# Expert and mixer weights as tiles with 16 KB per partition row, and the pools that hold them

## The chip, the core and the metric

The kernel runs on one core of one Trainium2 chip. The metric is the device time of one execution in microseconds (us); three executions before the change are shown. Times inside the kernel come from one profiled execution.

## What is computed

256 tokens of width 1024 pass through two blocks. The first block is a mixer (half a Hyena convolution, half a differential attention), and then a mixture of experts in which each of 16 experts picks its 32 tokens. Cut to what matters here, the reference's expert part is:

```
cap = EC_CAPACITY_FACTOR * L // N_EXPERTS      # 32
aff = jax.nn.softmax(logits, axis=-1)
g, idx = lax.top_k(aff.transpose(2, 0, 1), cap)
xin = h[bi, idx]
a = jnp.einsum('bcd,df->bcf', xe, wg)          # d 1024, f 2816, for each expert
u = jnp.einsum('bcd,df->bcf', xe, wu)
y = jnp.einsum('bcf,fd->bcd', jax.nn.silu(a) * u, wd)
```

The experts' weights are 16 x 3 x 1024 x 2816 values of float32, 554 MB, each used once. The second block (two layers: gated feed-forward, a mixer, a second feed-forward, a gated embedding) has some 180 MB of weights for all 256 tokens.

## The kernel before, in words

**Weight tiles.** All large weights come as tiles of 128 partitions x 2048 float32, 8 KB per partition and 1 MB per load, packed on the host so that a tile is contiguous in HBM. `load_w` (L125) takes a slot from the list `K.raws` (L119, the one taken longest ago) and issues one load on SP's queue (L131). A slot is free again when its last reader is done. For the mixers and the second block, `split_w` (L150) parts a tile into float32r high and low parts: ScalarE copies (L162), VectorE or GpSimd subtracts (L165), in two pieces of 1024 columns that go to slots of the pools `hl`, `hlf` and others; each product is then three matmuls (`mm3`, L182 to L184). The experts' weights are multiplied as they are, in float32.

**First mixers** (`pre` L800, `mixers` L844). The projection `w_in` is 6 blocks of 512 columns, two tiles each (half of the 1024 rows per tile); `weights(n)` (L922) fetches both. The first five tiles are fetched ahead (L866, L874), in between small tables. `w_out` is four tiles (L822). SBUF is two stacks, left and right. On the left lie `raw` (3 slots) and `rawx` (2 slots), then the pools of the mixers; when these are done, the right stack gets `rx` and `rawy` (NY = 12 slots, L813), and the first 12 expert tiles are fetched into it (L814); 4 more follow when `rawz1` (2 slots, L1109) opens.

**Experts** (`moe` L1103). Four quartets q of experts, and in each 11 chunks c of 256 features: 44 chunks. The 32 tokens of each of the four experts stand on 32 of 128 PSUM partitions, so that the four experts' matmuls (stationary 128 x 32, moving 128 x 512) stand side by side. A chunk loads 8 gate and up tiles (expert e, half h of the rows) and 4 down tiles (expert e), 12 MB. The order on TensorE is

```
for h in range(2):
    w = [K.load_w(("moe_gu", 4 * q + e, c, h)) for e in range(4)]
    for k in range(4):
        for e in range(4):
            ...
```

so the first product of a half needs the tiles of all four experts, and the four slots come free together (L1122 to L1128). Each `nc.tensor.matmul` of float32 is two instructions in the profile. Then ScalarE takes the SiLU (L1139), VectorE multiplies (L1140), TensorE transposes (L1144), and the down products follow (L1146 to L1151), again with the expert innermost. The router (L971) finds the tokens before; the pairs of k of the gathered tokens `xinT` (L1035) come one after another, and the first products are woven in between.

**Slots.** In quartets 0 to 2 the list holds 3 + 2 + 12 + 2, and from the first chunk on one more (`rawz`, L1135): 20 slots of 8 KB. At the start of quartet 3 (L1157) the right stack's pools close, `rawz` is closed and opened anew with one slot, and 8 slots stay; the room goes to tables of the second block's S5 layer, which are worked out in six parts behind the first six chunks (L1170 to L1175; VectorE L331 and others, TensorE L466 and L497, small transfers L473 from GpSimd's queue). Behind chunk 5 the tables' scratch closes and `rawz2` gives 4 more (L1178). At the end of a quartet the outputs are put back to their tokens (L1182 to L1190).

**Second block** (`second` L1654). It uses the 3 slots of `raw`, which have been there from the beginning. Its first step splits a feed-forward tile (L1659), its second is `final_norm` (L1200, ScalarE's square on L1209).

**Who orders what.** The order on each engine and in each queue follows the order of the program, except that the language's scheduler moves instructions and loads that are ready earlier ahead of others: the first expert tiles, for instance, go to free slots of `rawx` and `raw` before those of `rawy`. `issue_after` (L148, L1174) holds an instruction behind another.

## Time and profile before

| | us |
|---|---|
| three executions | 2633.45, 2632.69, 2639.59 |
| median | 2633.45 |
| profiled execution: span from first to last instruction | 2637.2 |
| profiled execution: what lies around the span | not listed |
| to the first expert products | about 228 |
| experts | 228 to 1536 |
| second block | 1536 to the end |
| TensorE busy (matmul) | 2168.1, 82% of the span |
| VectorE, ScalarE, GpSimd busy | 922.9, 627.2, 112.2 |

The span is read in stages, since a mean over stages with different limits says little: where the sixteen DMA engines are busy all the time, bytes count, and where TensorE is, instructions count. The groups of rows below are from the page of this execution and from queries of its trace. [...] SPq is SyncE's load queue.

### The profile page before, as it was taken

What the parts mean: (1) busy time and instruction counts of PE and PEld (TensorE: products, weight loads), DVE (VectorE), ACT (ScalarE), POOL (GpSimd) and SP (SyncE); (2) the same over time, 40 slices, a digit from 0 to 9 for tenths busy, and PEclk for the clock granted to TensorE, in tenths of its full rate; (3) what the DMA queues carried; (4) which work ended last, traced back from release to release, by engine and by line L of the source; (5) the groups of instructions that cost most, each with busy time, mean ns of one, the idle gap of its engine ahead of it and who ended that gap; (6) DMA issues with size and microseconds to landing.
All of it is one profiled execution on the core that took longest, in us unless ns stands there. A gap on an engine that the chain in (4) does not pass through costs nothing.

```text
span 2637.2 us, 26475 instructions
## 1 busy us (share of the span) xinstructions
PE 2168.1 (82%) x10570; PEld 1199.1 (45%) x10570; DVE 922.9 (35%) x1745; ACT 627.2 (24%) x966; POOL 112.2 (4%) x85
## 2 busy tenths in 40 slices
PE   7997767666767767676677689999999999899998
PEld 5763111111111111111122157778777777777776
DVE  6653000000000000002412055565754755686545
ACT  4421000000000000000000044443543544465443
POOL 1110000000000000000000010001000200100001
PEclk9998898999899898988888889999999999899999
DMA  5248999999999999999998975533654554344541
GB/s 204 98 170 346 421 420 420 421 421 420 421 420 420 420 421 420 420 394 421 421 361 357 422 292 189 185 119 121 250 190 146 192 192 180 128 160 150 189 164 44
DMA packets 108002, 761.68 MB, mean 289 GB/s; under 512 B 12343, under 2 KB 12648, under 8 KB 17240
## 3 DMA queue, kind: packets, MB, share of 16 engines
q1 hardware_dynamic: 107000, 757.60, 72.1%
q0 software_dynamic: 880, 2.40, 0.5%
q8 instruction: 83, 1.36, 0.2%
q14 instruction: 39, 0.32, 0.0%
HBM read 757.72 MB, written 1.05 MB: 288 GB/s over the span
## 4 chain that ended last, share of the span: by engine, by line
DMA 45%; PE 45%; DVE 7%; ACT 1%; issue 1%; SPq 0%; POOL 0%; DVEq 0%; ACTq 0%; POOLq 0%
DMA w<-in_moe_gu 29%; DMA w<-in_moe_d 16%; PE b_w L184 8%; PE b_w L182 8%; PE b_w L183 8%; PE b_y L182 3%; PE b_y L184 3%; PE b_y L183 3%; PE b_au L1127 2%; DVE wlo L165 1%; PE b_y L1149 1%; PE b_pj L183 1%; PE b_pj L184 1%; PE b_pj L182 1%; PE b_tr L1300 1%
## 5 line engine op out<-in xcount | busy, mean ns | idle before, releaser
L1127 PE MATMUL b_au<-w,xinT 128*32 128x512 f32 x2816 | 611.5, 729 | 282.6 <-DMA w<-in_moe_gu 282.4
L165 DVE TENSOR_TENSOR wlo<-w,whi 128x1024 fp32r<-128x1024 f32 (+2 forms) x354 | 427.0, 1213 | 239.9 <-ACT whi L162 233.2
L1127 PEld LDWEIGHTS b_au<-w,xinT 128*32 128x32 f32 x2816 | 123.2, 128 | 734.9 <-DMA w<-in_moe_gu 497.3
L162 ACT ACTIVATE whi<-w 128x1024 fp32r<-128x1024 f32 (+2 forms) x374 | 385.4, 1040 | 248.0 <-PE b_w L184 131.7
L1140 DVE SCALAR_TENSOR_TENSOR m_g<-b_au,rsg,m_g 128x256 f32<-128x256 f32 x44 | 21.3, 483 | 1101.2 <-ACT m_g L1139 1101.2
L182 PE MATMUL b_w<-whi,hT 128*128 128x512 f32 (+2 forms) x864 | 347.1, 402 | 1.4 <-ACT hT L254 0.8
L184 PE MATMUL b_w<-whi,hT 128*128 128x512 f32 (+2 forms) x864 | 341.1, 395 | 2.7 <-DVE hT L255 2.7
L183 PE MATMUL b_w<-wlo,hT 128*128 128x512 f32 (+2 forms) x864 | 340.1, 394 | 0.9 <-DVE wlo L165 0.9
L1149 PE MATMUL b_y<-w,m_gT 128*32 128x512 f32 x1408 | 294.2, 602 | 53.4 <-DMA w<-in_moe_d 32.6
L1139 ACT ACTIVATE m_g<-b_au,rsg 128x256 f32<-128x256 f32 x44 | 20.8, 473 | 1215.6 <-PE b_au L1127 1215.6
L184 PEld LDWEIGHTS b_w<-whi,hT 128*128 128x128 f32 x864 | 164.5, 190 | 40.0 <-DVE hT L255 5.3
L182 PEld LDWEIGHTS b_w<-whi,hT 128*128 128x128 f32 x864 | 165.3, 191 | 34.9 <-ACT hT L254 2.9
L183 PEld LDWEIGHTS b_w<-wlo,hT 128*128 128x128 f32 x864 | 164.9, 191 | 33.6 <-DVE wlo L165 1.9
L1149 PEld LDWEIGHTS b_y<-w,m_gT 128*32 128x32 f32 x1408 | 69.9, 109 | 237.9 <-issue 124.2
L184 PE MATMUL b_y<-whi,f_gT 128*128 128x512 f32 x352 | 139.6, 401 | 7.9 <-DVE f_gT L255 7.9
L182 PE MATMUL b_y<-whi,f_gT 128*128 128x512 f32 x352 | 145.9, 414 | 0.0
L183 PE MATMUL b_y<-wlo,f_gT 128*128 128x512 f32 x352 | 140.7, 400 | 0.0
L165 POOL TENSOR_TENSOR wlo<-w,whi 128x1024 fp32r<-128x1024 f32 (+1 forms) x20 | 48.1, 2415 | 1004.4 <-ACT whi L162 819.6
L184 PEld LDWEIGHTS b_y<-whi,f_gT 128*128 128x128 f32 x352 | 66.9, 192 | 32.6 <-DVE f_gT L255 17.9
L182 PEld LDWEIGHTS b_y<-whi,f_gT 128*128 128x128 f32 x352 | 67.0, 190 | 29.8 <-ACT f_gT L254 19.3
L183 PEld LDWEIGHTS b_y<-wlo,f_gT 128*128 128x128 f32 x352 | 67.2, 191 | 10.3
L255 DVE TENSOR_TENSOR f_gT<-b_tr,f_gT 128x256 fp32r<-128x256 f32 x88 | 37.0, 421 | 64.0 <-ACT f_gT L254 64.0
(535 smaller groups left out, 1917.4 us busy)
## 6 DMA issues: line engine op xcount, KB each, us to landing
w<-in_moe_gu SPq DMA_DIRECT2D x352, 1024.0 KB, 19.8
w<-in_moe_d SPq DMA_DIRECT2D x176, 1024.0 KB, 19.8
w<-in_ffn_gu SPq DMA_DIRECT2D x88, 1024.0 KB, 4.8
w<-in_ffn_d SPq DMA_DIRECT2D x44, 1024.0 KB, 4.8
w<-in_w_in SPq DMA_DIRECT2D x12, 1024.0 KB, 8.3
w<-in_ab_in SPq DMA_DIRECT2D x8, 1024.0 KB, 4.8
w<-in_ple_g SPq DMA_DIRECT2D x8, 1024.0 KB, 4.8
w<-in_w_out SPq DMA_DIRECT2D x4, 1024.0 KB, 5.0
```

The source lines that it names most:

```text
L162: nc.scalar.activation(hi, s, AF.Copy)
L165: (e or nc.vector).tensor_sub(lo, s, hi.bitcast(F32))
L182: mm(out, lh, rh, start=start, stop=False)
L183: mm(out, lh, rl, start=False, stop=False)
L184: mm(out, ll, rh, start=False, stop=stop)
L255: return self.nc.vector.tensor_sub(lo, src, hi.bitcast(F32)), i
L1127: nc.tensor.matmul(au[e * 32:(e + 1) * 32], xinT[:, h * 4 + k, s:s + 32], w[e][:, k * 512:(k + 1) * 512], start=h + k == 0, stop=h == 1 an ...
L1139: nc.scalar.activation(g, au[:, :256], AF.Silu, scale=r)
L1140: v.scalar_tensor_tensor(g, au[:, 256:], r, g, op0=ALU.mult, op1=ALU.mult)
L1149: mm = nc.tensor.matmul(y[n][e * 32:(e + 1) * 32], gT[:, f, e * 32:(e + 1) * 32], w[e][:, f * 1024 + n * 512:f * 1024 + (n + 1) * 512], st ...
L1300: nc.tensor.transpose(b[:, f * 128:(f + 1) * 128], g[:, f * 128:(f + 1) * 128], K.ident)
```

## The change

It makes the experts' and the first mixers' tiles twice as wide, 16 KB per partition and 2 MB per load. An expert tile now holds the same rows for all four experts of a quartet: a gate and up tile two values of k (256 of the 1024 rows), a down tile one of the two groups of 128 features. Every tile can so be multiplied as soon as it is there. A chunk has 4 + 2 loads in place of 8 + 4. `w_in` has one tile per block of columns, of which the first is loaded in two parts; `w_out` has two tiles. The pools change with it: `rawx` has 3 slots of 16 KB and lives until the experts are done, `rawy` 6, `rawz1` 1, `rawz` 1 from quartet 3 on, `rawz2` 2; `raw`, with 3 slots of 8 KB, opens only for the second block, under the pool `post`. GpSimd's scratch for its own DMA descriptors is cut to 4096 bytes per partition; nothing is named before, and the default is 16384. Lines that only change comments are left out.

```diff
-NY = 12
+NY = 6
...
-        self.add_raw(ctx.enter_context(self.pool("raw", raw_bufs)), raw_bufs)
+        self.cols = 2048
...
+    @contextmanager
+    def width(self, cols):
+        old, self.cols = self.cols, cols
+        yield
+        self.cols = old
...
-        return p.tile([128, 2048], F32, name="w")
+        return p.tile([128, self.cols], F32, name="w")
...
-    def load_w(self, key, cols=2048):
+    def load_w(self, key, cols=None, parts=1):
...
-        self.nc.sync.dma_start(t[:, :cols], src[key[1:]] if len(key) > 1 else src)
+        src = src[key[1:]] if len(key) > 1 else src
+        n = (cols or self.cols) // parts
+        for i in range(parts):
+            c = slice(i * n, (i + 1) * n)
+            self.nc.sync.dma_start(t[:, c], src[:, c])
...
-        n = cols // 2
+        cols = cols or self.cols
+        m = max(2, cols // 1024)
+        n = cols // m
         parts = ([], [])
-        for i in range(2):
+        for i in range(m):
             p = self.hls.pop(0)
...
             for h in (1, 0):
+                w = K.weight(("w_out", h))
                 for n in range(2):
-                    w = K.weight(("w_out", n, h))
...
-    K.prefetch([("w_in", 2, 0), ("w_in", 2, 1)])
+    K.prefetch([("w_in", 2)], parts=2)
...
-    K.prefetch([("w_in", 3, 0), ("w_in", 3, 1), ("w_in", 4, 0)])
+    K.prefetch([("w_in", 3), ("w_in", 4)])
...
     def weights(n):
-        return [K.weight(("w_in", n, h)) for h in range(2)]
+        return K.weight(("w_in", n))
...
-            K.prefetch([("w_out", n, h) for h in (1, 0) for n in range(2)])
+            K.prefetch([("w_out", h) for h in (1, 0)])
...
-        rz1.enter_context(K.more_raw("rawz1", 2))
+        rz1.enter_context(K.more_raw("rawz1", 1))
...
-            for h in range(2):
-                w = [K.load_w(("moe_gu", 4 * q + e, c, h)) for e in range(4)]
-                for k in range(4):
+            for k2 in range(4):
+                w = K.load_w(("moe_gu", q, c, k2))
+                for i in range(2):
+                    k = 2 * k2 + i
                     for e in range(4):
                         s = q * 128 + e * 32
-                        nc.tensor.matmul(au[e * 32:(e + 1) * 32], xinT[:, h * 4 + k, s:s + 32],
-                                         w[e][:, k * 512:(k + 1) * 512], start=h + k == 0, stop=h == 1 and k == 3)
+                        o = (2 * e + i) * 512
+                        nc.tensor.matmul(au[e * 32:(e + 1) * 32], xinT[:, k, s:s + 32], w[:, o:o + 512],
+                                         start=k == 0, stop=k == KT - 1)
...
-                rz.enter_context(K.more_raw("rawz", 13 - NY, last=True))
-            w = [K.load_w(("moe_d", 4 * q + e, c)) for e in range(4)]
+            w = [K.load_w(("moe_d", q, c, f)) for f in range(2)]
...
                     for e in range(4):
+                        o = e * 1024 + n * 512
                         mm = nc.tensor.matmul(y[n][e * 32:(e + 1) * 32], gT[:, f, e * 32:(e + 1) * 32],
-                                              w[e][:, f * 1024 + n * 512:f * 1024 + (n + 1) * 512],
-                                              start=c + f == 0, stop=c == NCH - 1 and f == 1)
+                                              w[f][:, o:o + 512], start=c + f == 0, stop=c == NCH - 1 and f == 1)
...
                     right.close()
-                    rz.close()
                     rz.enter_context(K.more_raw("rawz", 1))
...
-                    rz.enter_context(K.more_raw("rawz2", 4, last=True))
+                    rz.enter_context(K.more_raw("rawz2", 2, last=True))
...
-    K = Core(ctx, tc, raw_bufs=3)
+    K = Core(ctx, tc)
...
-    K.moe_first = ([("moe_gu", e, 0, h) for h in range(2) for e in range(4)] + [("moe_d", e, 0) for e in range(4)]
-                   + [("moe_gu", e, 1, 0) for e in range(4)])
-    rx = ExitStack()
-    rawx = rx.enter_context(K.pool("rawx", 2))
-    K.add_raw(rawx, 2)
-    right = ExitStack()
-    with K.more_hl("hl", 4):
-        pre(K, I, x, right)
+    K.moe_first = ([("moe_gu", 0, 0, k) for k in range(4)] + [("moe_d", 0, 0, f) for f in range(2)]
+                   + [("moe_gu", 0, 1, k) for k in range(2)])
     tbs = ExitStack()
-    S = moe(K, I, x, right, lambda: tbs.enter_context(K.pool("tb", side="right")))
-    K.drop_raw(rawx)
-    rx.close()
-    with K.pool("post") as p:
+    with K.width(4096), K.more_raw("rawx", 3):
+        right = ExitStack()
+        with K.more_hl("hl", 4):
+            pre(K, I, x, right)
+        S = moe(K, I, x, right, lambda: tbs.enter_context(K.pool("tb", side="right")))
+    with K.more_raw("raw", 3), K.pool("post") as p:
...
+def _moe_gate_up(g, u):
+    out = np.empty((4, NCH, 4, 128, 4, 2, 2, 256), g.dtype)
+    for i, w in enumerate((g, u)):
+        a = w.reshape(4, 4, 4, 2, 128, NCH, 256)
+        out[..., i, :] = a.transpose(0, 5, 2, 4, 1, 3, 6)
+    return out.reshape(4, NCH, 4, 128, 4096)
+def _moe_down(w):
+    a = w.reshape(4, 4, NCH, 2, 128, 1024)
+    return np.ascontiguousarray(a.transpose(0, 2, 3, 4, 1, 5)).reshape(4, NCH, 2, 128, 4096)
...
-    nc = bacc.Bacc("TRN2", target_bir_lowering=False, num_devices=1)
+    nc = bacc.Bacc("TRN2", target_bir_lowering=False, num_devices=1, dynamic_dma_scratch_size=4096)
```

`_wide`, not shown, packs `w_in` and `w_out` in the same way, [128, 4096] per tile.

## Rows read from the trace of the kernel before

**Rows 1.** The page: GB/s in 40 slices; the chain that ended last.
```profile
GB/s 204 98 170 346 421 420 420 421 421 420 421 420 420 420 421 420 420 394 421 421 361 357 422 292 189 185 119 121 250 190 146 192 192 180 128 160 150 189 164 44
...
DMA w<-in_moe_gu 29%; DMA w<-in_moe_d 16%; PE b_w L184 8%; PE b_w L182 8%; PE b_w L183 8%; PE b_y L182 3%; PE b_y L184 3%; PE b_y L183 3%; PE b_au L1127 2%; DVE wlo L165 1%; PE b_y L1149 1%; PE b_pj L183 1%; PE b_pj L184 1%; PE b_pj L182 1%; PE b_tr L1300 1%
```
**Rows 2.** Windows of the three stages.
```profile
0.00:228.00 228.00, 190.06 (x986) 138.49 (x986) 145.39 (x328) 84.78 (x148) 32.44 (x33) 0.94 0.47 179
228.00:1536.00 1308.00, 919.35 (x4547) 223.77 (x4546) 121.12 (x310) 28.92 (x60) 9.70 (x12) 0.91 1.00 412
1536.00:2637.00 1101.00, 1058.74 (x5039) 836.85 (x5038) 656.43 (x1108) 513.48 (x758) 70.07 (x40) 0.98 0.46 166
```
**Rows 3.** Windows: stretches of the expert stage.
```profile
222.00:231.00 9.00, 9.00 (x55) 4.14 (x58) 1.93 (x4) 1.42 (x3) 0.00 (x0) 0.80 0.01 2
231.00:1175.00 944.00, 658.37 (x3250) 155.07 (x3244) 43.10 (x100) 20.46 (x42) 4.06 (x4) 0.92 1.01 420
1175.00:1185.00 10.00, 9.43 (x38) 2.58 (x35) 1.74 (x3) 0.60 (x1) 0.73 (x1) 1.00 0.65 246
...
1345.00:1370.00 25.00, 14.76 (x80) 3.60 (x78) 5.14 (x21) 0.47 (x1) 4.92 (x8) 0.80 0.98 263
...
1410.00:1430.00 20.00, 15.86 (x82) 5.62 (x81) 9.36 (x10) 0.47 (x1) 0.00 (x0) 0.91 0.59 222
```
**Rows 4.** 300 to 600 us: DMA packets, issues (median to landing), SP's waits (total, times, longest).
```profile
DMA packets 17305, 126.13 MB, mean 420 GB/s; under 512 B 1916, under 2 KB 1916, under 8 KB 1916
w<-in_moe_gu SPq DMA_DIRECT2D x80, 1024.0 KB, 19.9
...
SPq L131 <- DMA w<-in_moe_gu: 169.4, 80, 3.4
SPq L131 <- DMA w<-in_moe_d: 83.9, 40, 2.1
```
**Rows 5.** DMA packets of 3 to 4.5 us, and of 11 to 14 us.
```profile
DMA packets 168, 0.62 MB, mean 415 GB/s; under 512 B 16, under 2 KB 16, under 8 KB 168
...
DMA packets 473, 1.16 MB, mean 388 GB/s; under 512 B 58, under 2 KB 93, under 8 KB 452
```
**Rows 6.** The page's group of gate and up products; weight loads near 1346; SP's issues (ns).
```profile
L1127 PE MATMUL b_au<-w,xinT 128*32 128x512 f32 x2816 | 611.5, 729 | 282.6 <-DMA w<-in_moe_gu 282.4
...
1346.02 0.13 PEld L1127 LDWEIGHTS b_au<-w,xinT 128*32 128x32 f32 x4 [0.30 <-issue]
1346.45 0.13 PEld L1127 LDWEIGHTS b_au<-w,xinT 128*32 128x32 f32 x4 [0.30 <-issue]
...
L131 SPq DMA_DIRECT2D w<-in_moe_gu x80: 327/328/328, 302.1 to 599.9; - x80
```
**Rows 7.** Timeline of SP, 222 to 232 us.
```profile
230.79 0.33 SPq L131 DMA_DIRECT2D w<-in_moe_gu  x1
```
**Rows 8.** Timeline, 1168 to 1192 us.
```profile
1179.08 3.62 PE L1149 MATMUL b_y<-w,m_gT 128*32 128x512 f32 x20 [0.57 <-DMA w<-in_moe_d]
...
1182.73 2.98 SPq L131 DMA_DIRECT2D w<-in_moe_gu  x6
```
**Rows 9.** SP's longest wait, 1400 to 1430 us; GpSimd's queue, 1345 to 1370 us.
```profile
SPq L131 <- DVE t_Vt L331: 14.3, 1, 14.3
...
q0 software_dynamic: 400, 1.18, 34.0%
```
**Rows 10.** Timeline, 1524 to 1560 us.
```profile
1532.53 3.62 PE L1149 MATMUL b_y<-w,m_gT 128*32 128x512 f32 x20 [0.63 <-DMA w<-in_moe_d]
...
1536.45 2.00 ACT L162 ACTIVATE whi<-w 128x1024 fp32r<-128x1024 f32 x2 [0.53 <-DMA w<-in_ffn_gu]
...
1538.83 1.06 ACT L1209 ACTIVATE hT<-x 128x1024 fp32r<-128x1024 f32 x1 [0.37 <-DVE x L1190]
```
**Rows 11.** ScalarE's wait, 4 to 40 us; the first reader of the S5 tables' transfers.
```profile
ACT whi L162 <- DMA w<-in_w_in: 2.8, 1, 2.8
...
L572 PE MATMUL b_s<-s_T,s_U x64: 272/284/298, 1768.8 to 1803.5; 128*32 128x128 f32 x64
```

More of the change, by code (lines that the diff above doesn't have):

```diff
@@ L54, with __init__ @@
 class Core:
-    def __init__(self, ctx, tc, raw_bufs=3):
+    def __init__(self, ctx, tc):
         self.tc = tc
@@ L103, in pool @@
         return self.tc.tile_pool(name=name, bufs=bufs, side=side, reuse_waits="tile")
-    def add_raw(self, pool, bufs):
-        self.raws = [pool] * bufs + self.raws
     @contextmanager
@@ L130, in load_w, with prefetch @@
         src = self.I[key[0]]
-        self.nc.sync.dma_start(t[:, :cols], src[key[1:]] if len(key) > 1 else src)
+        src = src[key[1:]] if len(key) > 1 else src
[3 more added lines that the diff above has]
+            self.nc.sync.dma_start(t[:, c], src[:, c])
         return t
-    def prefetch(self, keys):
+    def prefetch(self, keys, parts=1):
         for k in keys:
-            self.ahead[k] = self.load_w(k)
+            self.ahead[k] = self.load_w(k, parts=parts)
     @contextmanager
@@ L826, in pre @@
                             kk = h * 4 + k
-                            K.mm3(b[n, t], mix[0][:, kk, s], mix[1][:, kk, s], w[0][:, k * 512:(k + 1) * 512],
-                                  w[1][:, k * 512:(k + 1) * 512], h == 1 and k == 0, h == 0 and k == 3)
+                            ws = slice(n * 2048 + k * 512, n * 2048 + (k + 1) * 512)
+                            K.mm3(b[n, t], mix[0][:, kk, s], mix[1][:, kk, s], w[0][:, ws], w[1][:, ws],
+                                  h == 1 and k == 0, h == 0 and k == 3)
                         if h == 1:
@@ L907, in conv_part @@
             for k in range(KT):
-                s = slice((k % 4) * 512 + c * 128, (k % 4) * 512 + (c + 1) * 128)
-                K.mm3(b, w[k // 4][0][:, s], w[k // 4][1][:, s], hT[0][:, k], hT[1][:, k], k == 0, k == KT - 1)
+                s = slice(k * 512 + c * 128, k * 512 + (c + 1) * 128)
+                K.mm3(b, w[0][:, s], w[1][:, s], hT[0][:, k], hT[1][:, k], k == 0, k == KT - 1)
             if n < 2:
@@ L944, in mixers @@
                     for k in range(KT):
-                        s = slice((k % 4) * 512 + c * 128, (k % 4) * 512 + (c + 1) * 128)
-                        K.mm3(b, w[k // 4][0][:, s], w[k // 4][1][:, s], hT[0][:, k], hT[1][:, k],
-                              k == 0, k == KT - 1)
+                        s = slice(k * 512 + c * 128, k * 512 + (c + 1) * 128)
+                        K.mm3(b, w[0][:, s], w[1][:, s], hT[0][:, k], hT[1][:, k], k == 0, k == KT - 1)
                     nc.scalar.activation(qk[n][:, c], b, AF.Copy)
@@ L953, in mixers @@
                         s = slice(t * 128, (t + 1) * 128)
-                        ws = slice((k % 4) * 512, (k % 4 + 1) * 512)
-                        K.mm3(b, hT[0][:, k, s], hT[1][:, k, s], w[k // 4][0][:, ws], w[k // 4][1][:, ws],
-                              k == 0, k == KT - 1)
+                        ws = slice(k * 512, (k + 1) * 512)
+                        K.mm3(b, hT[0][:, k, s], hT[1][:, k, s], w[0][:, ws], w[1][:, ws], k == 0, k == KT - 1)
                     nc.scalar.activation(vn[:, t], b, AF.Copy)
@@ L1778, in layout @@
     o["x"] = i["x"].reshape(2, 128, 1024)
-    o["w_in"] = _tiles(i["w_in"][0])
-    o["w_out"] = _tiles(i["w_out"][0])
+    o["w_in"] = _wide(i["w_in"][0], 0)
+    o["w_out"] = _wide(i["w_out"][0], 1)
     o["filt_w1"], o["filt_w2"], o["filt_w3"] = i["filt_w1"][0], i["filt_w2"][0], i["filt_w3"][0]
```

12 lines of the change are left out of this document (8 added, 4 removed).

## The prediction

> **What bounds the kernel now.** I read the slices of the page first, then three stages by windows, then the expert stage in stretches, then who keeps SP's load queue waiting. The slices show a plateau of 420 GB/s from slice 4 to slice 23, and the chain that ended last consists there of loads of expert weights, 29% and 16% of the span [rows 1]. By stage the first mixers (to 228 us) and the second block (from 1536 us) load at 179 and 166 GB/s, while the expert stage, 1308 us, loads at 412 with the DMA engines' busy share at 1.00 and PE at 919 us of 1308 [rows 2]. So one stage is worth looking at, and in it the time is bytes over rate plus the moments at which the queue runs dry. The stretches show both: 420 GB/s from 231 to 1175, and four holes: 222 to 231, 1175 to 1185, 1345 to 1370 and 1410 to 1430 [rows 3]. In steady state SP waits for earlier loads to land, 120 times for 120 issues, and a 1 MB load lands 19.9 us after its issue [rows 4], which is eight loads of 2.49 us one behind another. PE is no rival bound: four matmuls, one for each expert, leave every 0.43 us, so that the 24 such groups of a chunk (2816 / 44 = 64 instructions of gate and up and half as many of down, four to a group) [rows 6] take 10.3 us of the 30 us that its 12 loads of 1.05 MB need at 420.
>
> **Part 1, the length of a row.** 528 loads of 128 rows of 8 KB become 264 of 128 rows of 16 KB; bytes stay. Each load also counts 16 packets under 512 B: 1916 of them for 120 loads in 300 us [rows 4]. What a packet costs beside its bytes is not shown by a row, so I bound it by a two-term model, 16 engines always busy: engine time = a times bytes + b times packets. The expert stage gives 4800 us = a x 126.13 MB + b x 17305 [rows 4]. At the program's start the queue is full too, with shorter rows: in 1.5 us, 24 us = a x 0.62 MB + b x 168, rows of 4 KB, and in 3 us, 48 us = a x 1.16 MB + b x 473, a mixture [rows 5]. The first pair gives b = 4.9 ns, the second 12.3 ns. One 2 MB load in place of two of 1 MB saves 144 packets, that is 144 x b / 16 = 0.044 or 0.111 us of 4.99. With ten slots filled ahead, 254 loads remain: 11 or 28 us. I take the middle, 19 us (427 GB/s), because the first stretch is purer and the second twice as long; the ends for the range are 0 (rate not moved by rows) and 28. [...]
>
> SP issues half as many loads, 0.33 us each [rows 6]; it waited between them anyway, so that is worth nothing. If SP's limit is eight loads, 16 MB may now be under way, and the ten slots limit first; the queue stays filled either way.
>
> **Part 2, the start.** From 222 to 231 the queue is dry, at 2 GB/s [rows 3]: all slots that exist then (3 + 2 + 12 + 2 of 8 KB, 19 MB) are full, and PE gives none back before 230.8 us [rows 7], because experts are innermost and four tiles end together. Afterwards 3 + 6 + 1 slots hold 20 MB: one MB less to load later, 2.5 us. A tile is done after two values of k, 16 matmul instructions, not after four values, 32; the first slot comes back at least four groups of 0.43 us earlier, and more if the products follow the gathering of tokens pair by pair. I take 3.5 us, together 6; ends 3 and 9 (the whole hole). The filling itself still waits for the mixers' pools; a coarser tile waits for the later of two neighbours, and a hole of 9 us covers that.
>
> **Part 3, the third boundary.** From 1175 to 1185 the rate is 246: a loss of 10 x (1 - 246/420) = 4.1 us. SP's next load leaves at 1182.7, just after the quartet's last down product [rows 8], because the slot of the reopened pool was the last one filled. Afterwards that pool is new at this point; it can touch a tile of the right-hand pool at most, and four tiles are loaded behind those. I take 4; ends 2 and 4.
>
> **Part 4, the S5 tables beside the last quartet.** From 1410 to 1430 the rate is 222, a loss of 9.4 us; SP's wait there ends on the tables' VectorE work, 14.3 us [rows 9], behind which PE's transposes and so the products stood. The eight slots are freed in fours: with four in use, 4 x 2.5 = 10 us of loads are under way, less than 14.3. Five slots of 2 MB, freed singly, leave four, 19.7 us. That covers the wait; I take 8, ends 4 and 9. The hole from 1345 to 1370 (a loss of 9.3 us) I leave: in it the POOL queue's small rows hold 34% of the engines' time, 8.5 us of 25 [rows 9], and these transfers stay as they are.
>
> **Part 5, the edges.** The last tile to land is now half of the down weights for all experts, 16 instructions, 1.7 us, where a run of 20 took 3.62 [rows 10]: up to 2 us. Against it, the second block's three slots are no longer older than the stage. By the order in which the seven slots rotate, they lie on tiles of which two hold the last down weights, so that the first feed-forward tile starts a little later; ScalarE splits it at 1536.45 and the norm's square is queued behind at 1538.83 [rows 10]. I set the edges at 0; ends -2 and 2. From there on the second block's pools and order are as before, PE is busy 1059 of 1101 us [rows 2], and I carry nothing over. In the first mixers the loads change from 12 to 7 and from 4 to 2, at 179 GB/s of use; ScalarE's only wait for them is 2.8 us at the first tile [rows 11], which is still loaded in two parts; the parts of a tile use the same four pairs of split buffers in the same order. If the split waited for both parts, 2.5 us would be lost; all four pieces are needed for the first sum over k anyhow, so 0. The POOL queue's scratch shrinks from 16 to 4 KB; if its eight table transfers stood longer, their reader comes at 1768.8 [rows 11], 400 us later: 0.
>
> **Sum.** 19 + 6 + 4 + 8 + 0 = 37 us. The profiled span is 2637.2 us and becomes 2600; what lies around the span is not listed for that execution, and the median of the three runs is 2633.45, 3.75 below the span. I carry the 37 us to the median: 2596. The ends sum to 7 and 52 us, 2626 and 2581.
>
> **Rivals.** (A) Rows do not matter: a 16 KB row is moved as two packets, or a limit of the source sets 420. Then 18 us remain: 2615. [...] For it: in the stage itself only one row length is seen. Against: 388 GB/s with short rows against 420 [rows 4, 5]. (B) The slots are too coarse: the holes at 1175 and 1410 stay because SP issues in order and one 2 MB slot held by PE stops all behind it. Then 25 us: 2608. For it: the hole of 1410 came from just such a held slot. Against: the count of MB under way behind it. (C) Slower: a row of 16 KB lowers the rate, for instance by 16 engines walking HBM in steps twice as large. The stage's 1308 us grow by 1% for each 1% of rate; with the other 18 us it turns slower than the bound once the rate falls below 420 x (1 - 26/1308) = 412 GB/s. At 404, halfway to the lowest full-queue rate seen, it would be 52 - 18 = 34 us more: 2667. Against: every step up in row length so far raised the rate. (D) The stage ends 37 us earlier but the second block starts into a wait on reused memory and gives most of it back: 2630. Against: only two slots are touched.
>
> **How the numbers follow.** Forecast 0.56, A 0.22, B 0.11, C 0.07, D 0.04. A measurement of this kernel can tell about 0.3%, 8 us, from no change. Forecast, A and B are faster by more than that, 0.88 with small remainders; D counts as same, 0.05; C is slower, 0.07. The range from 2582 to 2622 takes in A, B and nearly all of the forecast's ends; C, D and the far tails are left out.
>
> **What would show it.** Right: packets of 16 KB (about half as many per 300 us), the stretch after the start at 425 to 430 GB/s, loads landing after some 40 us, no hole near 1175, little of the one near 1410, and the last down product about 37 us earlier, with the time from there to the end unchanged within 3 us. Wrong: 420 GB/s with half the packets (A); SP waiting for PE with the engines idle in the last quartet (B); a plateau under 412 (C); a later first product of the second block relative to the last expert product (D).

## The result, and the profile after

The changed kernel takes 2608.17 us (median of 4 runs, 2607.12 to 2608.98); beside them the kernel before took 2636.12 us (4 runs, 2632.69 to 2639.59). The ratio is 0.9896 with a 95% interval of 0.9877 to 0.9914: faster by 28 us where 37 were forecast, inside the range. The span of the profiled execution goes from 2637.2 to 2606.4 us, 30.8 less; in the later executions the time is some 1.8 us more than the span, so that the profiled one of before took about 2639, some 3 us over its median, and the one of after took its median. Medians and ratios below leave out slow executions: one of ten of e1_rows8k (4489.60 us) and two of four of e2_halfloads (3592.68 and 3694.98 us).

The page of the kernel after: GB/s in 40 slices, and the chain that ended last.

```profile
GB/s 223 98 146 369 427 427 427 428 427 427 428 428 427 427 427 428 427 426 429 427 355 415 423 228 185 182 114 164 214 192 130 210 194 171 143 144 166 180 175 33
...
DMA w<-in_moe_gu 30%; DMA w<-in_moe_d 15%; PE b_w L194 8%; PE b_w L193 8%; PE b_w L192 8%; PE b_y L192 3%; PE b_y L194 3%; PE b_y L193 3%; PE b_au L1138 2%; DVE wlo L175 1%; PE b_y L1160 1%; PE b_pj L192 1%; PE b_pj L193 1%; PE b_pj L194 1%
```

The plateau stands at 427 instead of 420, the dip at slice 18 (394 in [rows 1]) is gone, and slices 21 to 23, 361 357 422 before, are 355 415 423. The bound is the same: loads of expert weights take 45% of the chain in both.

From 300 to 600 us of the kernel after: packets, then the waits of SP (total, times, longest).

```profile
DMA packets 8809, 128.25 MB, mean 427 GB/s; under 512 B 981, under 2 KB 981, under 8 KB 981
...
w<-in_moe_gu SPq DMA_DIRECT2D x41, 2048.0 KB, 39.2
...
SPq L139 <- DMA w<-in_moe_gu: 181.8, 40, 5.6
SPq L139 <- DMA w<-in_moe_d: 94.5, 21, 4.5
```

Half as many packets as in [rows 4] carry 1.7% more bytes. A load of 2 MB lands 39.2 us after its issue: again eight loads, now 16 MB, one behind another at 2 x 2.453 = 4.91 us each.

Windows of the kernel after. The columns, here and in [rows 2] and [rows 3], are the stretch, its length, busy time and number of instructions of TensorE (PE), its weight loads (PEld), VectorE (DVE), ScalarE (ACT) and GpSimd (POOL), the granted TensorE clock as a share of full speed, the DMA engines' mean busy share, and GB/s. The stretches are the expert stage, the third boundary, which comes earlier here, then the places of the three later holes.

```profile
228.00:1500.00 1272.00, 769.71 (x4541) 175.88 (x4543) 121.47 (x310) 28.37 (x59) 9.74 (x12) 0.77 1.00 422
...
1150.00:1185.00 35.00, 24.22 (x122) 5.45 (x122) 4.85 (x8) 1.55 (x3) 0.00 (x0) 0.75 1.01 428
1175.00:1185.00 10.00, 7.28 (x32) 1.19 (x32) 0.48 (x1) 0.47 (x1) 0.00 (x0) 0.50 1.01 429
1320.00:1360.00 40.00, 20.76 (x141) 5.99 (x139) 6.34 (x22) 0.47 (x1) 4.94 (x8) 0.69 1.01 308
1380.00:1400.00 20.00, 6.88 (x32) 5.43 (x32) 12.67 (x12) 0.00 (x0) 0.00 (x0) 0.57 0.94 388
```

The hole at the boundary is gone. The one of the S5 transfers lies earlier and is no smaller: 40 x (1 - 308/427.5) = 11.2 us lost, against 9.3. (The rate counts the transfers' own 1.18 MB, which would take 2.8 us at 427.5; for the loads of weights the loss is 14.0 us.) Of the last one 20 x (1 - 388/427.5) = 1.8 us are left, against 9.4.

Timeline of the kernel after: SP's first issue after the start, the last products of the expert stage, and the passage into the second block.

```profile
229.31 2.85 SPq L139 DMA_DIRECT2D w<-in_moe_d  x2
...
1494.43 1.92 PE L1160 MATMUL b_y<-w,m_gT 128*32 128x512 f32 x16 [0.52 <-DVE m_gT L1155]
...
1498.72 3.59 PE L1160 MATMUL b_y<-w,m_gT 128*32 128x512 f32 x16 [2.37 <-DMA w<-in_moe_d]
...
1506.59 0.14 DVE L221 TENSOR_SCALAR rd_m<-x_ss 128x1 f32<-128x1 f32 x1
...
1507.77 2.93 ACT L172 ACTIVATE whi<-w 128x1024 fp32r<-128x1024 f32 x3
...
1508.77 3.51 DVE L1223 SCALAR_TENSOR_TENSOR x<-x,rd_r,s_ga 128x512 f32<-128x512 f32 x2
1508.89 5.61 POOL L175 TENSOR_TENSOR wlo<-w,whi 128x1024 fp32r<-128x1024 f32 x2 [180.05 <-DVE rs_t L210]
...
1512.20 2.30 DVE L214 SCALAR_TENSOR_TENSOR rs_y<-rs_t,rs_y 128x1 f32<-128x1 f32 x1
...
1518.88 0.78 PE L192 MATMUL b_w<-whi,hT 128*128 128x512 f32 x1
```

The same timeline of the kernel before: its first expert product, GpSimd's lower halves, the norm's operations, the second block's first product.

```profile
222.24 1.92 PE L1127 MATMUL b_au<-w,xinT 128*32 128x512 f32 x2
...
1537.60 4.68 POOL L165 TENSOR_TENSOR wlo<-w,whi 128x1024 fp32r<-128x1024 f32 x2 [185.67 <-ACT whi L162]
...
1540.43 0.14 DVE L211 TENSOR_SCALAR rd_m<-x_ss 128x1 f32<-128x1 f32 x1
...
1541.29 1.00 DVE L204 SCALAR_TENSOR_TENSOR rs_y<-rs_t,rs_y 128x1 f32<-128x1 f32 x1
...
1542.64 0.16 DVE L204 SCALAR_TENSOR_TENSOR rs_y<-rs_t,rs_y 128x1 f32<-128x1 f32 x1
...
1543.41 1.40 DVE L1214 SCALAR_TENSOR_TENSOR x<-x,rd_r,s_ga 128x512 f32<-128x512 f32 x2
...
1549.33 0.78 PE L182 MATMUL b_w<-whi,hT 128*128 128x512 f32 x1
```

The last expert product ends at 1498.72 + 3.59 = 1502.31 instead of 1536.15 ([rows 10]: 1532.53 + 3.62), 33.8 us earlier. From there to the second block's first product, **the edge**, it takes 16.6 us where it took 13.2: 3.4 are given back. The rest of the span is 1087.5 and was 1087.9.

**Where the 30.8 us come from.** Rate: 1 MB (1.0486 x 10^6 bytes) took 2.494 us [rows 4] and takes 2.453; for the 508 MB that are loaded after the start that is 20.9. Start: SP re-issues 1.5 us earlier (229.31 against 230.79 [rows 7]) and one MB more lies ahead, 2.5: together 4.0. Boundary 4.1. Last hole 9.4 - 1.8 = 7.6. S5 transfers 9.3 - 11.2 = -1.9. Edge -3.4. Second block 0.4. These make 31.7; 0.9 us I can't assign.

### The profile page after: what moved, and what is told of

Its sections match the earlier page's. It is cut to its first block, busy times and chain, and to the rows that moved or that the text cites. A ratio compares the mean times of both kernels' runs of the same rounds, so it can differ in the third digit from the quotient of the medians.

```text
span 2606.4 us, 25947 instructions
## 1 busy us (share of the span) xinstructions
PE 2015.9 (77%) x10570; PEld 1147.7 (44%) x10570; DVE 926.8 (36%) x1745; ACT 627.0 (24%) x966; POOL 113.2 (4%) x85
## 4 chain that ended last, share of the span: by engine, by line
PE 45%; DMA 45%; DVE 7%; ACT 1%; issue 1%; POOL 0%; SPq 0%; DVEq 0%; ACTq 0%; POOLq 0%
DMA w<-in_moe_gu 30%; DMA w<-in_moe_d 15%; PE b_w L194 8%; PE b_w L193 8%; PE b_w L192 8%; PE b_y L192 3%; PE b_y L194 3%; PE b_y L193 3%; PE b_au L1138 2%; DVE wlo L175 1%; PE b_y L1160 1%; PE b_pj L192 1%; PE b_pj L193 1%; PE b_pj L194 1%; PE b_tr L1309 1%
## 5 line engine op out<-in xcount | busy, mean ns | idle before, releaser
L1138 PE MATMUL b_au<-w,xinT 128*32 128x512 f32 x2816 | 470.6, 801 | 326.6 <-DMA w<-in_moe_gu 326.5
L1138 PEld LDWEIGHTS b_au<-w,xinT 128*32 128x32 f32 x2816 | 92.6, 129 | 695.8 <-DMA w<-in_moe_gu 412.1
L1160 PE MATMUL b_y<-w,m_gT 128*32 128x512 f32 x1408 | 245.4, 834 | 117.7 <-DMA w<-in_moe_d 101.3
L1149 ACT ACTIVATE m_g<-b_au,rsg 128x256 f32<-128x256 f32 x44 | 20.9, 474 | 1178.6 <-PE b_au L1138 1178.6
L1160 PEld LDWEIGHTS b_y<-w,m_gT 128*32 128x32 f32 x1408 | 47.3, 133 | 268.7 <-DMA w<-in_moe_d 127.3
L1154 PE MATMUL b_tr<-ident,m_g 128*128 128x128 f32 x88 | 22.0, 337 | 49.3 <-DVE m_g L1150 49.3
```

Of the source, the lines that this page charges most:

```text
L1138: nc.tensor.matmul(au[e * 32:(e + 1) * 32], xinT[:, k, s:s + 32], w[:, o:o + 512], start=k == 0, stop=k == KT - 1)
L1149: nc.scalar.activation(g, au[:, :256], AF.Silu, scale=r)
L1154: nc.tensor.transpose(b[:, f * 128:(f + 1) * 128], g[:, f * 128:(f + 1) * 128], K.ident)
L1160: mm = nc.tensor.matmul(y[n][e * 32:(e + 1) * 32], gT[:, f, e * 32:(e + 1) * 32], w[f][:, o:o + 512], start=c + f == 0, stop=c == NCH - 1 ...
```

## The experiments

To read the runs, each trace is cut at three rows of its timeline: start of the first gate and up product, end of the last down product, start of the second block's first product. Between the first two lies the **stage**, between the last two the **edge**. All times in us; the ratio is to the kernel before on the same chip, with its 95% interval. Stage and edge are of the one profiled execution of each kernel, and do not count when its first product starts: at 222.2 to 223.1 us in most, but at 227.7 in e4_one_by_one, 224.4 in e6_no_st, 225.0 in e11_st_flat and 225.5 in e13_st_late.

| kernel | median | ratio | stage | edge |
|---|---|---|---|---|
| before | 2636.12 | 1 | 1313.9 | 13.2 |
| after | 2608.17 | 0.9896 [0.9877, 0.9914] | 1279.8 | 16.6 |
| e1_rows8k | 2629.45 | 0.9965 [0.9953, 0.9976] | 1299.6 | 17.3 |
| e2_halfloads | 3490.63 (2 runs) | 1.3231 [1.3111, 1.335] | | |
| e3_rows4k | 2662.44 (1 run) | | 1335.5 | 17.3 |
| e4_one_by_one | 2631.14 | 0.9977 [0.9965, 0.9988] | 1304.7 | 16.6 |
| e9_rows_only | 2657.87 | 1.0069 [1.0046, 1.0092] | 1324.7 | 16.6 |
| e7_after_again | 2607.32 | 0.9889 [0.9869, 0.9908] | 1278.7 | 16.6 |
| e8_split_first | 2609.21 | 0.9896 [0.9879, 0.9913] | 1279.7 | 16.7 |
| e5_rawz_last | 2609.12 | 0.9893 [0.9877, 0.991] | 1280.4 | 16.6 |
| e6_no_st | 2593.18 | 0.9841 [0.9818, 0.9864] | 1272.6 | 17.8 |
| e11_st_flat | 2618.14 | 0.9901 [0.9884, 0.9917] | 1288.1 | 17.1 |
| e12_flat_dve | 2615.48 | 0.9894 [0.988, 0.9909] | 1288.9 | 15.3 |
| e13_st_late | 2604.32 | 0.9878 [0.9857, 0.9899] | 1265.7 | 15.3 |

**Rows: 8 KB, 4 KB, and half the partitions.** The edits of the changed kernel, in `load_w`:

```diff
+        if key[0] in ("moe_gu", "moe_d"):
+            parts = 2                     # e1_rows8k; 4 in e3_rows4k
...
+            for i in range(2):            # e2_halfloads
+                r = slice(i * 64, (i + 1) * 64)
+                self.nc.sync.dma_start(t[r], src[r])
+            return t
```

> The changed kernel, but each expert tile of 2 MB comes by two loads, one for the left half of its columns and one for the right: rows of 8 KB as before the change, in the new slots and in the new order of products. Theory (a packet is one row, and each packet costs the transfer engines a fixed time besides its bytes): between 300 and 600 us the packets go back to some 17,300, the rate from 427 to 420 GB/s, and the run is 18 to 22 us slower than the changed kernel, about 2629 us. Rival (the gain comes from fewer or larger tiles and slots, not from the rows): the rate stays at 427 and the run within 4 us of 2608.

> The changed kernel with each expert tile loaded by four loads of a quarter of its columns each: rows of 4 KB, four times the packets. Theory (a fixed time per packet, the same at every length): from 16 KB to 8 KB the stage took 0.041 us more for each MB-tile, so 4 KB adds three times as much: 0.124 us on 2.453, some 407 GB/s between 300 and 600 us with about 33,500 packets, and the run some 63 us slower than the changed kernel, about 2670 us. Rival (the cost is no fixed time per packet but a step at some length, or engines that hide it when packets are short): 415 to 420 GB/s as with 8 KB, 2625 to 2640 us; or far worse, under 395 GB/s and over 2695 us.

> The changed kernel, but each expert tile comes by two loads of 64 partitions each, whose rows keep their 16 KB: as many loads as in the run with 8 KB rows, as many packets as in the changed kernel. Theory (packets cost, loads don't): 427 GB/s and some 8,800 packets between 300 and 600 us, 2608 us within 4. Rival (each load has a cost of its own at its start or end): the rate falls towards 420 GB/s as with 8 KB rows, and the run is 10 to 22 us slower than the changed kernel.

The packets of 300 to 600 us, in this order of the three kernels:

```profile
DMA packets 17310, 126.15 MB, mean 420 GB/s; under 512 B 1920, under 2 KB 1920, under 8 KB 1920
```
```profile
DMA packets 33682, 122.76 MB, mean 409 GB/s; under 512 B 3739, under 2 KB 3739, under 8 KB 33672
```
```profile
DMA packets 5089, 66.66 MB, mean 222 GB/s; under 512 B 1020, under 2 KB 1020, under 8 KB 1020
```

With 8 KB rows the rate is that of before to the third digit, though slots and order are those of after, and the stage is 19.8 us longer: the rate follows the row. With 4 KB rows 1 MB takes 300/122.76 x 1.0486 = 2.562 us, 0.110 more than with 16 KB where 0.124 was expected; from 64 to 128 packets per MB that is 0.64 ns of the stage for each packet, from 64 to 256 packets 0.57. So the cost is close to a fixed time per row: 16 engines work side by side, 9 to 10 ns of one engine each (8 to 9 if the 16 small packets of each load are counted too, as the prediction did). The stage is 55.7 us longer than after; the 63 expected were 13% too many.

Shorter rows came with more loads here, and in these figures a cost of each load would look the same. The packets' own times tell the two apart: in the median of 300 to 600 us a packet of 16 KB takes 614 ns (after), one of 8 KB 313 (e1_rows8k) and one of 4 KB 162 (e3_rows4k). Two halves take 12 ns more than the whole, four quarters 34, some 11 to 12 ns for each row more. That covers the whole loss, and nothing is left for a cost of each load.

The loads of 64 partitions were to tell packets from loads, and told something else: both theories fell. The rate halves, from 427 to 222 GB/s. The engines are as busy as ever (100.9% of the 16 engines' time from 300 to 600 us, 100.5% in the kernel after), but a 16 KB packet takes twice as long, 1233 ns in the median, when each load writes only 64 partitions; on average 4800 us of engine time over 5089 - 1020 packets are 1.18 us, against 4800 / (8809 - 981) = 0.61. The same run loads at 251 to 309 GB/s between some 900 and 1520 us. Why writing 64 partitions at a time halves the rate, and why it costs less there, no run shows.

**Single tiles, and rows, each alone.** In the kernel before, each 1 MB tile is packed so that it can be multiplied alone; in the kernel after, each 2 MB tile holds one expert (down: two), so that four are needed at once, as before.

```diff
-            for h in range(2):                                                # e4_one_by_one
-                w = [K.load_w(("moe_gu", 4 * q + e, c, h)) for e in range(4)]
+            for k in range(KT):
+                w = K.load_w(("moe_gu", q, c, k))
...
-            for k2 in range(4):                                               # e9_rows_only
-                w = K.load_w(("moe_gu", q, c, k2))
+            w = [K.load_w(("moe_gu", q, c, e)) for e in range(4)]
+            for k in range(KT):
```

> The kernel before, with its pools, its 8 KB rows and its 1 MB tiles, but each tile packed so that it can be multiplied alone: a gate and up tile holds one of the eight k for all four experts, a down tile one of the four pairs of f and n. Theory (the gain has two parts): the rate between 300 and 600 us stays at 420 GB/s; the hole at 1175 to 1185 us is gone (4 us), the hole at 1410 to 1430 us is mostly gone (up to 8 us), the first re-issue comes a microsecond or two earlier; in all 8 to 16 us faster than before, 2620 to 2628 us. Rival 1 (the single tiles give all of the gain): 25 us or more faster. Rival 2 (they give nothing without the larger rows): within 3 us of before, the holes where they were.

> The changed kernel with its slots and its 16 KB rows, but a gate and up tile holds one expert with all eight k, a down tile two experts: the first product of a chunk needs all four tiles, as before the change. Theory (rows and single tiles add up): 427 GB/s between 300 and 600 us; the holes of before come back or are larger, since four tiles are now 8 of the 16 MB that the slots hold: 8 to 20 us slower than the changed kernel, 2616 to 2628 us. Rival (the slots' new layout closed the holes, whatever the tiles hold): within 3 us of 2608.

Windows of the run with single 1 MB tiles: boundary, S5 transfers, last hole.

```profile
1175.00:1185.00 10.00, 6.59 (x37) 1.60 (x38) 2.38 (x4) 0.60 (x1) 0.00 (x0) 1.00 0.62 230
...
1350.00:1380.00 30.00, 13.22 (x70) 1.77 (x62) 4.45 (x19) 0.48 (x1) 2.82 (x5) 0.62 1.02 274
...
1410.00:1430.00 20.00, 12.33 (x94) 3.96 (x92) 9.28 (x11) 0.47 (x1) 0.00 (x0) 0.97 0.94 370
```

The same of the run with 16 KB rows, four tiles needed at once: the stage, and around the boundary.

```profile
228.00:1500.00 1272.00, 780.65 (x4356) 195.84 (x4348) 118.92 (x305) 27.18 (x57) 9.76 (x12) 0.78 0.97 407
...
1175.00:1195.00 20.00, 10.77 (x64) 2.44 (x62) 0.93 (x4) 0.47 (x1) 0.00 (x0) 0.83 0.67 266
```

Single tiles alone shorten the stage by 9.2 us: the last hole shrinks from 9.4 to 2.4 us, and SP's first re-issue follows the first product after 4.7 us (232.41 - 227.73) instead of 8.6. But the hole at the boundary stays (4.5 us), against the expectation. Nor do the new slots close it alone: without single tiles 20 x (1 - 266/427.5) = 7.6 us are lost there. With both it is gone, with 8 KB rows too (e1_rows8k runs at 422 GB/s in the same window). The run as a whole gains less than the 8 to 16 us expected, 0.23%: its first product comes 5.5 us later in the profiled execution (the slowest of its ten), and its edge is 16.6 us too, so the longer edge needs neither the 16 KB rows nor the new slots.

Rows and slots without single tiles have the full 427 GB/s from 300 to 600 us, and are still 10.8 us slower in the stage than before, 44.9 slower than after; the expectation was 8 to 20. The loss begins at the boundary, from where only five slots of 2 MB are left for tiles that are needed in fours. So the parts don't add up: single tiles are worth 9.2 us in the old slots and 44.9 in the new ones. **They are what makes five slots of 2 MB bearable here.**

**The edge.** Once in ScalarE's order, once in the order of the slots:

```diff
+        with K.tc.issue_after(K.pre_hi.ins):        # e8_split_first: Square behind the split
             j = nc.scalar.activation(hi[:, :, t * 128:(t + 1) * 128], ...
...
-                    rz.enter_context(K.more_raw("rawz", 1))
+                    rz.enter_context(K.more_raw("rawz", 1, last=True))       # e5_rawz_last
```

> The changed kernel itself, unaltered, timed beside the next three on one chip so that differences of 2 to 4 us can be read. Every theory: 2606 to 2610 us, ratio to before 0.988 to 0.991; the last products of the expert stage again end some 34 us earlier than before, and the second block starts 16 to 17 us after them.

> The changed kernel with one order forced: ScalarE makes the upper halves of the second block's first weights (L172) before its two Squares (L1218), as in the kernel before, instead of after them. Theory (the 3.4 us that the change lost between the last expert product and the second block are VectorE's norm operations standing still while GpSimd makes the lower halves): GpSimd's two lower halves start at about 1504 instead of 1508.9 us and are done near 1509, VectorE's norm operation that took 3.51 us for two takes about 1.4 again, and the second block starts 13 to 14.5 us after the last expert product: 2 to 4 us faster than the changed kernel. Rival (the weights land late, and the order doesn't matter): within 1 us of the changed kernel, with ScalarE waiting for the load before its Squares.

> The changed kernel, with the one slot that is added at the boundary of the last group of experts put at the end of the slots' order instead of at its head. The last chunk's tiles then lie otherwise, and the second block's first two weight slots overlay tiles that are freed earlier, so its first load is issued earlier and ScalarE's split stands ahead of its Squares without being forced. Theory: the edge of 16.6 us shrinks to 13 to 14 us, the expert stage's length stays within 1 us, 2 to 4 us faster than the changed kernel. Rival (the slot at the end of the order is filled later, so that less lies ahead at the boundary): the hole at 1175 to 1185 us comes back, 2 to 4 us, and the run is at 2606 to 2610 us.

The kernel timed again came as forecast. But a changed order gave nothing, twice. ScalarE's split in the run with the forced order, and VectorE's norm behind it:

```profile
1506.00 2.00 ACT L173 ACTIVATE whi<-w 128x1024 fp32r<-128x1024 f32 x2 [3.94 <-PE b_au L1198]
...
1509.08 0.15 DVE L223 TENSOR_SCALAR rd_m<-x_ss 128x1 f32<-128x1 f32 x1 [2.43 <-ACT hT L1221]
...
1509.95 1.89 DVE L216 SCALAR_TENSOR_TENSOR rs_y<-rs_t,rs_y 128x1 f32<-128x1 f32 x1
```

It was not late by order, and not by its load either: it waited 3.9 us for TensorE's last products of the stage, which put the outputs back to their tokens (that its output tile overlays what these read is the likely reason, and only argued); with the Squares behind it the edge stays at 16.7 us. In the second run the load left some 14 us earlier (1482.36), ScalarE's order had turned by itself, and the split waited 4.4 us for the same products. In the kernel before the split waited only for its load, at 1536.45 [rows 10], and ran while the outputs were put back.

What the 3.4 us are, VectorE's rows tell. In both kernels its norm begins 4.3 us after the last expert product (1540.43 - 1536.15 and 1506.59 - 1502.31). Before, GpSimd has more than half of its lower halves done by then, and only one of VectorE's operations is held up, 1.00 us instead of 0.16. After, the split and so GpSimd's lower halves come later, at 1508.89, beside the norm, and two are held up: 3.51 instead of 1.40, and 2.30 instead of 0.16. That is 4.25 us against 0.84, which makes the 3.4. So the first half of the theory was right, the stand-still beside GpSimd; what fell is the cure. With the split forced ahead, which still waits for the put-back, one operation is held up (1.89 us, 0.9 more than before), but the Squares behind it let the norm begin only 6.8 us after the last expert product, 2.5 later: 3.4 again.

**The S5 transfers.** Left out; then with unbroken rows; then this with the second block's first lower halves on VectorE instead of GpSimd; at last through HBM and later.

```diff
-        gp.dma_start(S.T[s * 16:(s + 1) * 16, :, s * 16:128], KT_[:, :, 0:128 - 16 * s])   # e6_no_st
...
+        gp.dma_start(Tf[s * 16:(s + 1) * 16, s * 16:4096], Kf[:, 0:4096 - 16 * s])         # e11_st_flat
...
-    K.presplit([("ffn_gu", 0, 0, 0, 0)], K.nc.gpsimd)                        # e12_flat_dve, e13_st_late
+    K.presplit([("ffn_gu", 0, 0, 0, 0)])
...
+    gp.dma_start(S.KD, KT_)                                                  # e13_st_late
...
+    with K.tc.issue_after(K.ha_op.ins):
+        for s in range(8):
+            K.nc.gpsimd.dma_start(S.T[s * 16:(s + 1) * 16, :, s * 16:128], S.KD[:, :, 0:128 - 16 * s])
```

> The changed kernel without the eight transfers that lay the S5 tables' responses into S.T (their reader finds zeros, so that part of the S5 layer's output is left out). Theory (the stretch at 1325 to 1355 us, at 254 to 293 GB/s, is lost to these 1.18 MB in small pieces that hold the transfer engines): that stretch runs at 425 GB/s or more, and the run is 8 to 12 us faster than the changed kernel. Rival 1 (the stretch is lost to the engine waits around it, SyncE behind the products): the stretch stays below 350 GB/s and the run within 3 us. Rival 2 (hidden by what is late next, the hole of the next part of the tables): the stretch is full but less than 5 us come out.

> The changed kernel with another way to lay out S.T: each of the eight transfers writes one unbroken row on each of its 16 partitions (all 32 groups, shifted as a whole) instead of 32 pieces of 64 to 512 B, and VectorE afterwards multiplies what spilled over a group's edge by 0, two operations behind the last part of the tables, where it is idle. 1.97 MB instead of 1.18 MB. Theory (the small pieces cost the engines, not the bytes): at 427 GB/s these bytes are some 5 us, so that of the 11 to 12 us lost at 1325 to 1355 us 5 to 8 come back; 4 to 10 us faster than the changed kernel, ratio to before 0.985 to 0.987. Rival 1 (writing to 16 partitions at a time is what costs, as the loads to 64 partitions showed): no gain or a loss up to 8 us, and the stretch as low as before. Rival 2 (TensorE's table products at the lower clock, then late slots, make the hole whatever the transfers do): the stretch falls towards 0 GB/s, SyncE waiting for the gate and up products for over 20 us, and the run within 3 us of the changed kernel.

> The run with the unbroken rows of S.T, and besides the lower halves of the second block's first weights worked out by VectorE in its own order instead of by GpSimd. Theory (VectorE's operations with two inputs in SBUF stand still while GpSimd reads SBUF; the two waits in the changed kernel's edge were about 2.1 us each): VectorE pays two operations of about 1.2 us and none waits, so the time from the last expert product to the second block's first goes from 16.6 to 13.5 to 15.5 us; the run 1 to 3 us faster than the one with unbroken rows alone. Rival (the edge is set by when ScalarE's split can begin, since its tiles lie on what the stage reads last): the edge stays at 16 to 17 us, the run within 1 us of the other.

> The changed kernel with S.T laid out later: behind the tables one transfer of 256 KB puts the responses into a buffer in HBM, and the eight transfers into S.T read it from there, issued behind the first norm of the second block, some 250 us ahead of S.T's first reader; besides, VectorE instead of GpSimd makes the lower halves of the second block's first weights, as in the run before. Theory (transfers that read and write only 16 partitions cost some 10 us of the queues' time for each MB, and this costs nothing where the queues are idle half of the time): of the 11 to 12 us lost at 1325 to 1355 us 2 to 4 stay, the edge is 15 to 15.5 us instead of 16.6, the second block is as long as before; 8 to 12 us faster than the changed kernel, 2595 to 2600 us, ratio to before 0.983 to 0.986. Rival 1 (the loads of the second block's weights wait behind these transfers): TensorE waits for weights at 1520 to 1560 us, up to 11 us, and the run is at 2604 to 2610 us. Rival 2 (the hole is there without the transfers, by slots that come free late): SyncE waits over 20 us for the gate and up products at 1315 to 1345 us, and less than 4 us come out.

Without the transfers the median is 14.1 us below that of the changed kernel timed beside it, more than the 8 to 12 expected, and as much as the loads lost with the transfers' own bytes counted (14.0). The time is lost to them. (Its profiled execution was its slowest, 2601.82 us, and its trace doesn't show the full stretch that was expected, for a reason told in the last section; the other three took 2591 to 2594. That the stretch fills when the transfers are gone is shown by e13_st_late.)

Unbroken rows don't help: the ratio is 0.9901 against 0.9889 of the changed kernel, and the stage is 8 to 9 us longer than in either trace of that. The stretch of this run, and of the one with later transfers:

```profile
1320.00:1360.00 40.00, 14.23 (x91) 3.62 (x89) 5.53 (x22) 0.47 (x1) 3.87 (x8) 0.66 1.01 232
```
```profile
1320.00:1360.00 40.00, 30.17 (x229) 13.74 (x231) 23.74 (x36) 0.47 (x1) 0.51 (x1) 0.87 1.01 423
```

With 2.07 MB in 256 packets 40 x (1 - 232/427.5) = 18.3 us are lost, with 1.18 MB in 400 packets 11.2: it goes by bytes, 9 us for each MB, and not by pieces. That is what the first rival said, 16 partitions at a time. With the transfers' own bytes the loads lost 18.3 + 4.8 = 23.1 us and 11.2 + 2.8 = 14.0, 11 to 12 us for each MB. In the last run the 256 KB that read 16 partitions but write to HBM cost 40 x (1 - 423/427.5) = 0.4 us, so it is the writing side.

VectorE in GpSimd's place takes the edge from 17.1 to 15.3 us, as expected; the run is 2.7 us faster, which is not clear of noise. This is VectorE there:

```profile
1518.02 0.74 DVE L1231 SCALAR_TENSOR_TENSOR x<-x,rd_r,s_ga 128x512 f32<-128x512 f32 x1
1518.68 2.35 DVE L175 TENSOR_TENSOR wlo<-w,whi 128x1024 fp32r<-128x1024 f32 x2
...
1520.95 0.75 DVE L1231 SCALAR_TENSOR_TENSOR x<-x,rd_r,s_ga 128x512 f32<-128x512 f32 x1
```

VectorE gives 2.35 us of work for the 4.25 of standing still, 1.9 less, and the edge is 1.8 shorter. The norm's two operations take 0.74 and 0.75 us; in the kernel after they took 3.51 together, and the next one of that kind 2.30 instead of 0.16, up to the end of a GpSimd operation (1512.20 + 2.30 = 1514.50 = 1508.89 + 5.61). The kernel before shows the same: the one operation held up there ends with GpSimd's (1541.29 + 1.00 = 1542.29, 1537.60 + 4.68 = 1542.28), while the norm's first, which has one input, took 0.14 us beside GpSimd at 1540.43, as in the kernel after, where GpSimd had not begun (1506.59). All the operations that were held up have two inputs in SBUF.

With the transfers moved, the holes of the S5 tables are gone, and the stage is 14.1 us shorter than after, the edge 1.3. But the run gains only some 3 us: its ratio of 0.9878 lies within the intervals of after. Rival 1 came true. The waits of that run between 1500 and 1560 us:

```profile
PE b_tr L1310 <- DVE f_g L1307: 9.4, 1, 9.4
...
ACT whi L173 <- DMA w<-in_ffn_d: 7.6, 1, 7.6
ACT whi L173 <- DMA w<-in_ffn_gu: 6.6, 2, 3.8
```

ScalarE's splits wait for the second block's first loads, as they don't in the kernel after, and behind them stand VectorE and TensorE; from its first product on the second block takes 1098.5 us instead of 1087.5. The 11 us were moved, not saved. (In this execution the first expert product came 3.0 us later than in that of after; 14.1 + 1.3 - 11.0 - 3.0 = 1.4 is what the spans differ by.) A later place, where no load of the second block is waited for, was not tried. This version is the fastest that computes the whole output, by less than can be told from the changed kernel.

## Why the prediction was right, and where it was off

- **What bounds it**: right. The expert stage is bytes over rate plus dry moments, and all of the gain lies there.
- **Part 1, rows**: right in kind and size: 19 us, measured 20.9 by the rate and 19.8 by e1_rows8k. The time per packet, taken between 4.9 and 12.3 ns, is 8 to 9 by the same count. That the middle of two figures so far apart was right is luck. Rival A (rows don't matter) is refuted: 427 GB/s with 16 KB rows, 420 with 8 KB, 409 with 4 KB.
- **Part 2, start**: 6 us, measured 4.0. The term that was mis-sized is the earlier return of the first slot, 3.5, which is 1.5. It was taken above its least value, 1.7, because the products wait for the gathered tokens pair by pair; but the gathering ends at 229.7 us before and 229.9 after, and before, 18 of the first tile's 32 products were done by then and the rest ran without a break.
- **Part 3, boundary**: 4 us, measured 4.1. The reason given, the new order of the slots, is half of it: single tiles in the old slots keep the hole, and so do the new slots without single tiles.
- **Part 4, S5 tables**: the last hole gives 7.6 of the 8. Leaving the other hole at its 9.3 us missed a small term: it grew by 1.9, and no run shows why. I put the hole down to the share of small rows in the engines' time; the runs show that it goes by the bytes that are written to 16 partitions at a time, 11.2 us for 1.18 MB and 18.3 for 2.07.
- **Part 5, edges**: the step that failed. It was set at 0 (-2 to 2) and came out at -3.4 on the edge itself. I looked at the slots of the second block's loads, and not at what else the split has to wait for, TensorE's last products, nor at where GpSimd's share of it would then fall: beside the norm, whose operations it holds up by 4.25 us instead of 0.84. And the 2 us hoped for at the last tile came to nothing in the profiled execution, as its 16 products took 3.59 us, not 1.7. Rival D, a wait on reused memory, is near to this at a tenth of its price. e4_one_by_one has the longer edge in nearly the old layout, with its split behind the first Square; so the layout alone doesn't decide when the split runs, and what does there is open.
- **Rival B** (coarse slots keep the holes): not for this change, but it is just what happens without single tiles, e9_rows_only. That the measured time is the 2608 that this rival gave is an accident: the holes that it kept are gone. Rival C (a lower rate with long rows) found nothing.

Of the 37 us, 35.7 were in the steps as they were read after the run (20.9 + 4.0 + 4.1 + 7.6 - 0.9 unassigned); what is missing is the edge and the growth of the hole that I had left alone, 5.3 together. The rest of the miss against 2596 is that a sum read from an execution of about 2639 us was carried to a median of 2633.45; the medians of before in all later comparisons lie between 2634 and 2643.

## What to carry to other kernels

Where loads bound a stage, count packets: with 128 partitions, doubling the row from 8 to 16 KB was worth 1.7% of the rate here. A tile twice as large paid here only because it can be used, and freed, by itself. Look also at how many partitions a transfer writes: small ones to 16 partitions held up the whole queue of loads, in both places where they were put ahead of loads that someone waits for: 11.2 us in the expert stage, 11.0 in the second block (e13_st_late). And look at what GpSimd runs beside VectorE at a seam between two stages: in the kernel after it made the edge 3.4 us longer.

## What the runs showed of the hardware

- Halving the partitions of a load halved the rate (427 to 222 GB/s between 300 and 600 us) at the same row length, the engines as busy (100.9% of the 16 engines' time, 100.5% in the kernel after). I had expected no effect or a few per cent.
- TensorE's granted clock, as a share of full speed, moves between 0.5 and 1 in this stage, in which it waits for loads: in the kernel after it was 1.00 during the 16 products from 1494.43 us, which took 1.92 us, and 0.52 during the last 16, from 1498.72, which took 3.59. It differs between kernels with equal work: 0.77 on average after, 0.91 before [rows 2], 0.95 with the same tiles loaded in two halves.

```profile
228.00:1500.00 1272.00, 856.80 (x4470) 196.90 (x4468) 120.58 (x308) 27.93 (x58) 9.75 (x12) 0.95 1.01 415
```

That is the stage of e1_rows8k; it is no faster for it, as loads bound it. In these runs the clock costs only where others wait for TensorE: the last 16 products took 3.59 us in one profiled execution and 1.92 in the other of the same kernel (1499.46 us in e7_after_again). In the profiled execution of e6_no_st the tables' products met the lower level, a granted clock of 0.50 where the kernel after had 1.00. Here are the stretch and the products in the kernel after, then in e6_no_st, and then SP's waits from 1310 to 1420 us there:

```profile
1311.00:1322.00 11.00, 11.00 (x129) 9.46 (x126) 4.75 (x7) 0.00 (x0) 0.00 (x0) 1.00 1.01 427
...
L476 PE MATMUL b_s<-s_X,t_Bre x64: 269/269/280, 1311.2 to 1322.0; 64*16 64x128 f32 x64
```
```profile
1311.00:1322.00 11.00, 11.00 (x65) 6.72 (x58) 2.04 (x3) 0.00 (x0) 0.00 (x0) 0.50 1.01 427
1322.00:1333.00 11.00, 11.00 (x70) 7.79 (x69) 2.71 (x4) 0.00 (x0) 0.00 (x0) 0.50 0.65 277
...
L476 PE MATMUL b_s<-s_X,t_Bre x64: 392/417/418, 1312.6 to 1333.1; 64*16 64x128 f32 x64
...
SPq L139 <- PE b_au L1136: 47.5, 13, 23.7
```

They end 11 us later, the chunk's products and so its slots come late, SP waits up to 23.7 us for them, and the stretch runs dry without any transfer in it. This is the mechanism of rival 1 of that run's expectation, in the one execution of its four that was profiled and was the slowest; that the clock was the cause is read from this one trace, and the other three left none.
